# Gate and up products by Strassen's seven quarter products, with the activations kept in DRAM, in a two-layer diffusion block

## The chip, the cores and the metric

The kernel runs on one core of a Trainium2 chip. The core has a matrix engine (TensorE, PE in the views; its weight loads are PEld), a vector engine (DVE), a scalar engine (ACT), a third elementwise engine (GpSimd, POOL), a queue engine that issues transfers (SyncE, SP), a bank memory for matrix results (PSUM) and a scratch memory (SBUF). The metric is the device time of one launch in microseconds (us); lower is better.

## The reference, cut to what matters

Two layers on 512 latent tokens and 256 context tokens, D_MODEL 1024, D_FF 2816, all in float32. The change concerns the feed-forward part and what lies right before and behind it:

```python
for l in range(DEPTH):                       # 2 layers
    mod = silu_c @ w_ada[l] + b_ada[l]       # shift, scale, gate (twice each)
    ...                                      # norm, projections, two attentions, merge, output projection
    h2 = modulate(rms_norm(x, norm2_g[l]), sh2, sc2)
    x = x + gt2 * swiglu(h2, w_ffn_gate[l], w_ffn_up[l], w_ffn_down[l])
    if not last:
        ...                                  # the same for the context tokens, with the same weights
return rms_norm(x, final_norm_g)

def swiglu(h, w_gate, w_up, w_down):
    return (jax.nn.silu(h @ w_gate) * (h @ w_up)) @ w_down
```

In the second layer only the 512 latent tokens pass the feed-forward part; in the first all 768 do.

## The kernel before, in words

Features lie across partitions and tokens along the free dimension, so an activation is a list of tiles of 128 features by 768 (layer 0) or 512 tokens (layer 1). Every matrix operand is split into a high and a low part, and `mm3` (L564) makes each product of a 128x128 weight block with a piece of tokens from three matmuls: high tokens with low weights (L569), low with high (L570), high with high (L571). In the page the token operand is `hh, hl` (normed input) or `ah, al` (activation), the weights are `wh, wl`, the result bank is `d`.

Instructions are issued in the order in which the program emits them. `defer` (L160) puts an emission off until the matrix engine has been handed a given amount of further work, counted by `pe` (L155).

Weights come through `Weights` (L41): tiles of 128 output features by 1024 (or 896) inputs are loaded over SP's queue into one of three buffers with the tag `wf` (L60), split on ACT (`wh`, L70) and DVE (`wl`, L71); each `get` splits two tiles ahead and loads a third.

The modulation columns are worked out in the background. `ada` (L446) loads a 512 KB tile of w_ada, named `wa`, **into the same three `wf` buffers**, and leaves one or two dot products on DVE (L455, L456: one for the latent condition, a second one where the context needs it too). `background` (L169) issues the dots of the tile loaded last and then the load of the next, `rate` times for each weight tile; called with a count it empties the list. In layer 0's feed-forward part the list has 56 tiles with 80 dots.

The feed-forward part is the second half of `rest` (L1055). The norm before it is made in two token halves: statistics (`st`, `rv`, `rr`, `rb`), then for each of eight feature tiles a product on DVE (`t`, L520), scale and shift on POOL (L531), the high part on ACT (L536) and the low part on DVE (L539). `norm` (L542) spreads these steps over matrix work. Then D_FF is walked in three groups of 7, 7 and 8 feature tiles (`GROUPS`): for every tile 8 input tiles by gate and by up (`ev_gate`: silu on ACT, L1126; `ev_up`: product on DVE, L1129, then split, L176 and L177), and behind a group its share of the down products, one weight tile for each of 8 output tiles, added to the residual stream `x` in SBUF by DVE (L1084). The last group runs in two token halves, so that the norm of the next layer can begin. Token pieces are 384 wide in layer 0; in layer 1 they are 512 wide but for the first three jobs of the feed-forward part and the last down group, which go by 256.

Of the kernel before, what the change touches and what calls it, by code (L numbers as in the profile page):

```python
# [32 lines left out]
ADA_RATE = 0.35  # L33
EPS = 1e-6
# [6 lines left out]
class Weights:  # L41
    """Streams weight tiles from DRAM in the order of use and splits each into two F32R parts."""
# [71 lines left out]
def drain(gen):  # L114
    for _ in gen:
        pass


class Kernel:
# [33 lines left out]
    # Instructions are issued in the order they are emitted: work that waits for another engine  # L153
    # is put off until the tensor engine has been given enough else to do.
# [25 lines left out]
    def weight_order(self, l):  # L180
# [11 lines left out]
        for _ in range(2):  # L192
            for m in range(8):
                W.add(a["w_out"][l, m])
        for g, (f0, fn) in enumerate(GROUPS):
            for f in range(2 * f0, 2 * (f0 + fn)):
                W.add(a["w_gu"][l, f])
# [4 lines left out]
    def run(self):  # L202
        nc, a = self.nc, self.a
        self.xg = self.tc.dram_tile([16, P, TOK], F32, name="gate_scratch")
        self.xs = self.tc.dram_tile([KD, P, SEQ], F32, name="x_scratch")
# [26 lines left out]
        self.cos = self.const("cos", [P, SEQ])  # L232
        self.sin = self.const("sin", [P, SEQ])
        self.mask = self.const("mask", [P, 5 * P])
# [14 lines left out]
    def first(self, tiles, fourth):  # L249
        """The first norm of layer 0, its shift and scale (on the tensor engine, in halves of four  # L250
        feature tiles) and three weight tiles with the contraction outermost."""
# [15 lines left out]
        def follow(i):  # L267
# [4 lines left out]
            if i == len(parts) - 1:  # L272
                for t, src in ((self.cos, "cos"), (self.sin, "sin"), (self.mask, "mask")):
                    nc.sync.dma_start(out=t, in_=self.a[src])
# [171 lines left out]
    def ada(self, l, f, both):  # L446
        """One tile of 128 modulation features; returns the arithmetic, to be issued once the tile is there."""
# [11 lines left out]
    def ada_scale(self, l, j, s):  # L459
        """norm gain * (1 + scale), in place of the scale columns."""  # L460
# [4 lines left out]
    def square(self, k, c0, c1, eng=None):  # L465
        """Adds up the squares of the feature tiles; the last one may be left for stats() to add."""
# [15 lines left out]
    def rstd_cols(self, ps, n, width, out):  # L482
        """1 / sqrt(ps / width + eps) of [P, n] sums."""
# [5 lines left out]
    def stats(self, c0, c1):  # L489
        """1 / rms of the tokens c0..c1, tokens across partitions."""  # L490
# [11 lines left out]
    def spread(self, r, c0, c1):  # L502
        """The same, along the free dimension of every partition."""
# [38 lines left out]
    def norm(self, l, j, c0, c1, pace):  # L542
        """The same, spread over the tensor engine's next work."""
# [55 lines left out]
    def dense_first(self, tiles):  # L599
        """Three weight tiles, the early chunks of all of them first: tiles of (chunks, evac)."""  # L600
# [21 lines left out]
    def head_stats(self, sq, n, r):  # L622
        """1 / rms of each of two heads' 64 rows, tokens across partitions: r [P, tiles * 2]."""
# [643 lines left out]
```

## Time and profile before

| what | us |
|---|---|
| median of 3 runs (1930.03 to 1935.9) | 1931.82 |
| span of the profiled execution | 1932.0 |
| busy in it: PE / DVE / ACT / POOL | 1880.6 / 1169.8 / 847.7 / 523.7 |
| layer 0, feed-forward stretch looked at (600 to 1155): PE busy | 555.00 |
| layer 1, the same (1582 to 1904): PE busy | 322.00 |

The profiled execution lies 0.2 us from the median, so its times can be set against the runs as they are. A stretch in which PE is busy for its full length has no gap between matmuls; DVE, ACT and POOL then work beside it.

### The profile page before, as it was taken

How to read it: one execution, taken by the hardware profiler on the slowest of the kernel's cores; microseconds unless marked ns; L12 is line 12 of the kernel's file. 1: busy time of each engine (PE TensorE's matmuls, PEld its weight loads, DVE VectorE, ACT ScalarE, POOL GpSimd, SP SyncE). 2: the span in 40 equal slices, each digit the busy share in tenths (PEclk: the TensorE clock that was granted, in tenths of full speed). 3: DMA queues.
4: the chain of work that ended last, by engine and by line, in shares of the span. 5: the costliest groups of instructions: out<-in, count | busy, mean ns of one | idle time of the engine just before them, and what ended most of it. 6: DMA issues, size and time to landing. Idle time of an engine off the chain costs nothing.

```text
span 1932.0 us, 29203 instructions
## 1 busy us (share of the span) xinstructions
PE 1880.6 (97%) x11248; PEld 1758.6 (91%) x11248; DVE 1169.8 (61%) x2095; ACT 847.7 (44%) x1607; POOL 523.7 (27%) x568
## 2 busy tenths in 40 slices
PE   7999999999999999999999999999999999999998
PEld 3889899988999999999999998888889998888887
DVE  7668868996556567545444457676886653333344
ACT  5458745776334221221122334774885442222233
POOL 3436636562234000000000144654651320000003
PEclk8999999999999999999999999999999999999999
DMA  8232332224442434443433451212116533333334
GB/s 289 90 96 80 93 104 86 80 71 170 139 145 87 120 118 137 129 130 124 149 121 123 130 164 57 75 50 75 62 34 202 181 110 92 105 94 103 93 109 137
DMA packets 67739, 219.89 MB, mean 114 GB/s; under 512 B 7649, under 2 KB 9729, under 8 KB 67473
## 3 DMA queue, kind: packets, MB, share of 16 engines
q1 hardware_dynamic: 60416, 204.30, 34.1%
q10 hardware_dynamic: 6992, 13.64, 1.9%
q8 instruction: 89, 1.46, 0.3%
q0 software_dynamic: 192, 0.08, 0.1%
q14 instruction: 50, 0.40, 0.1%
HBM read 203.32 MB, written 14.68 MB: 113 GB/s over the span
## 4 chain that ended last, share of the span: by engine, by line
PE 73%; POOL 1%; DVE 1%; ACT 1%; issue 1%; POOLq 0%; ACTq 0%; DVEq 0%
PE d L570 20%; PE d L571 20%; PE d L569 20%; PE av L834 2%; PE pr L571 2%; PE pr L569 2%; PE pr L570 2%; PE pt L823 2%; PE S L759 1%; PE S L760 1%; POOL t L531 0%; PE st L497 0%; PE S L762 0%; PE S L763 0%; DVE wl L71 0%
## 5 line engine op out<-in xcount | busy, mean ns | idle before, releaser
L569 PE MATMUL d<-hh,wl 128*128 128x384 f32 (+2 forms) x1728 | 614.2, 355 | 0.6 <-DVE q L845 0.4
L570 PE MATMUL d<-hl,wh 128*128 128x384 f32 (+2 forms) x1728 | 603.1, 349 | 1.5 <-DVE hl L539 1.3
L571 PE MATMUL d<-hh,wh 128*128 128x384 f32 (+2 forms) x1728 | 602.6, 349 | 0.0
L71 DVE TENSOR_TENSOR wl<-wf,wh 128x1024 fp32r<-128x1024 f32 (+1 forms) x221 | 272.5, 1234 | 274.6 <-ACT wh L70 273.8
L70 ACT ACTIVATE wh<-wf 128x1024 fp32r<-128x1024 f32 (+1 forms) x255 | 265.6, 1042 | 283.2 <-PE d L571 176.3
L570 PEld LDWEIGHTS d<-hl,wh 128*128 128x128 f32 x1728 | 326.7, 189 | 19.2 <-DVE hl L539 3.2
L571 PEld LDWEIGHTS d<-hh,wh 128*128 128x128 f32 x1728 | 325.7, 188 | 19.9
L569 PEld LDWEIGHTS d<-hh,wl 128*128 128x128 f32 x1728 | 326.4, 189 | 17.8 <-issue 0.9
L480 POOL TENSOR_TENSOR ssq<-ssq,sq 128x384 f32<-128x384 f32 (+1 forms) x48 | 68.5, 1428 | 879.7 <-ACT sq L476 865.3
L569 PE MATMUL d<-ah,wl 128*128 128x384 f32 (+2 forms) x592 | 197.7, 334 | 0.0
L571 PE MATMUL d<-ah,wh 128*128 128x384 f32 (+2 forms) x592 | 197.4, 333 | 0.0
L570 PE MATMUL d<-al,wh 128*128 128x384 f32 (+2 forms) x592 | 197.4, 333 | 0.0
L455 DVE SCALAR_TENSOR_TENSOR junk<-wa,crow 128x1024 bf16<-128x1024 f32 x128 | 159.2, 1244 | 0.0
L808 POOL TENSOR_SCALAR p<-p,rec 128x768 f32<-128x768 f32 (+3 forms) x160 | 131.4, 834 | 94.7 <-DVE rec L805 65.8
L1084 DVE SCALAR_TENSOR_TENSOR x<-d,mod,x 128x384 f32<-128x384 f32 (+3 forms) x144 | 70.8, 510 | 135.3 <-PE d L571 135.3
L176 ACT ACTIVATE ah<-s 128x384 fp32r<-128x384 f32 (+2 forms) x68 | 37.4, 551 | 248.2 <-DVE s L1129 248.2
L864 DVE TENSOR_TENSOR pt<-pt,pt 128x512 fp32r<-128x512 f32 (+1 forms) x192 | 123.9, 661 | 25.3 <-ACT pt L860 23.9
L860 ACT ACTIVATE pt<-pt 128x512 fp32r<-128x512 f32 (+1 forms) x192 | 107.3, 577 | 32.2 <-PE pt L823 28.0
L823 PE MATMUL pt<-ident,p 128*128 128x128 f32 x736 | 110.7, 275 | 6.0 <-POOL p L808 3.2
L570 PEld LDWEIGHTS d<-al,wh 128*128 128x128 f32 x592 | 111.7, 189 | 4.4
L569 PEld LDWEIGHTS d<-ah,wl 128*128 128x128 f32 x592 | 111.7, 189 | 4.4
L1126 ACT ACTIVATE s<-d 128x384 f32<-128x384 f32 (+2 forms) x68 | 35.1, 517 | 183.5 <-PE d L571 183.4
(172 smaller groups left out, 3168.8 us busy)
## 6 DMA issues: line engine op xcount, KB each, us to landing
wa<-w_ada SPq DMA_DIRECT2D x96, 512.0 KB, 3.6
wf<-w_gu SPq DMA_DIRECT2D x88, 512.0 KB, 3.6
wf<-w_in SPq DMA_DIRECT2D x52, 512.0 KB, 3.6
wf<-w_out SPq DMA_DIRECT2D x32, 512.0 KB, 3.6
wf<-w_dn SPq DMA_DIRECT2D x32, 512.0 KB, 3.6
wf<-w_dn SPq DMA_DIRECT2D x32, 448.0 KB, 3.4
wf<-w_proj SPq DMA_DIRECT2D x16, 512.0 KB, 3.8
x<-x SPq DMA_DIRECT2D x16, 384.0 KB, 5.1
```

The lines of the kernel that those rows point to most:

```text
L70: high = lambda: self.nc.scalar.activation(hi[:, :n], t[:, :n], AF.Copy)
L71: low = lambda: (engine or (self.nc.vector if self.aux is None else self.nc.gpsimd)).tensor_tensor(lo[:, :n], t[:, :n], hi[:, :n], ALU.sub ...
L455: nc.vector.scalar_tensor_tensor(junk, t, 1.0, self.crow[:, s, :], ALU.mult, ALU.mult, accum_out=acc)
L480: (eng or nc.gpsimd).tensor_tensor(self.ssq[:, c0:c1], self.ssq[:, c0:c1], t[:, c0:c1], ALU.add)
L569: nc.tensor.matmul(ps, wl[:, ks], xh[:, c0:c1], start=first, stop=False)
L570: nc.tensor.matmul(ps, wh[:, ks], xl[:, c0:c1], start=False, stop=False)
L571: nc.tensor.matmul(ps, wh[:, ks], xh[:, c0:c1], start=False, stop=last)
L808: nc.gpsimd.tensor_scalar(pt, pt, rec[:, i:i + 1], 1.0, ALU.mult, ALU.mult)
L823: nc.tensor.transpose(ps[:, o:o + P], u["p", i][:, (j0 + j) * P:(j0 + j + 1) * P], self.ident)
L860: nc.scalar.activation(r[1][0], r[0], AF.Copy)
L864: nc.vector.tensor_tensor(r[1][1], r[0], r[1][0], ALU.subtract)
L1084: nc.vector.scalar_tensor_tensor(x[:, b0:b1], ps[:, b0 - c0:b1 - c0], self.mod[l][s][:, gate:gate + 1], x[:, b0:b1], ALU.mult, ALU.add)
```

## The change

For both layers (`FAST`), the gate and up products of one feature tile f are taken together as a 2x2 block product: rows gate and up, inner halves of 512 inputs, columns the two token halves. Strassen's scheme (in Winograd's form) needs seven quarter products in place of eight, and sums on both sides. The token side (T1 to T4) is made once in `norm_fast`, at the end of the norm's second half; the weight side (S1 to S4, named `S`, `wh/wl`, `sh/sl`, `zh/zl`) for every f on DVE, POOL and ACT; the results are combined from the banks on DVE and ACT. The matrix work of f is `q6, r7, q5, p1, p2, p3, r4`; for the first four f (`EARLY`) the two plain gate products come first, by `Weights`, the other five later. A quarter product is 4 inner blocks by 3 matmuls, 384 wide in layer 0 and 256 wide in layer 1.

The activation of each f is stored to DRAM (`act_scratch`), and so is `x` (`x_scratch`); all 22 f run before any down product. Then `down` loads `x` and the activations again, splits them, and runs the three down groups. `project` leaves `rate` at 0 and `gate_up` does not raise it; `down` sets it to 2 in layer 0. The emptying call ahead of the last group stays.

```diff
+FAST = (True, True)
+EARLY = 4
...
+        if FAST[l]:
+            for f in range(EARLY):
+                W.add(a["w_gu"][l, 2 * f])
...
+    def norm_fast(self, l, n, half, c0, c1):
...
+            t0 = self.t0
+            for i in (0, 4, 1, 5, 2, 6, 3, 7):
+                times(i, rb)
+                affine(i)
+            J = range(4)
+            for j in J:
+                nc.vector.tensor_tensor(t[j], t[j], t[j + 4], ALU.subtract)
+                nc.vector.tensor_tensor(t0[j], t[j], t0[j], ALU.subtract)
+                high("T2", j, t0[j])
+            for j in J:
+                low("T2", j, t0[j])
+                high("T3", j, t[j])
...
+            for j in J:
+                low("T4", j, t0[j + 4])
...
+    def gate_up(self, l, last, n, tq):
...
+        def prep_s(f):
+            if f < NF:
+                s = S[f]["S"] = self.xa.tile([P, 1024], F32, name=self.nm("S"), tag="S", bufs=1)
+                G, U = S[f]["G"], S[f]["U"]
+                nc.vector.tensor_tensor(s[:, :512], U[:, :512], U[:, 512:], ALU.add)
+                nc.vector.tensor_tensor(s[:, 512:], G[:, :512], U[:, :512], ALU.add)
+
+        def prep_s2(f):
+            if f < NF:
+                G, s = S[f]["G"], S[f]["S"]
+                nc.gpsimd.tensor_tensor(G[:, :512], G[:, :512], s[:, :512], ALU.add)
+                nc.gpsimd.tensor_tensor(G[:, 512:], G[:, 512:], G[:, :512], ALU.add)
...
+        first(0, 0)
+        for f in range(EARLY):
+            if f + 1 < EARLY:
+                first(f + 1, 0)
+            first(f, 1)
+        self.flush()
...
+            prep_s(0)
+            prep_s2(0)
+            prep_24(0)
+            load(2)
+            prep_13(0)
+            prep_s(1)
+            prep_s2(1)
+            prep_24(1)
+            q6(0)
+            r7(0)
+            ev_sum(0, "u")
...
+    def down(self, l, last, n, chunks, halves, streams):
+        nc = self.nc
+        self.xt = []
+        for m in range(8):
+            x = self.unit("x")
+            nc.sync.dma_start(out=x[:, :n], in_=self.xs[m][:, :n])
+            self.xt.append(x)
...
+        acts = []
+        for f in range(2):
+            load(f)
+        for f in range(GROUPS[0][1]):
+            load(f + 2)
+            ready(f)
+        self.rate = 0 if last else 2
+        for g, (f0, fn) in enumerate(GROUPS):
+            act, acts = acts[:fn], []
...
+            def step(m):
+                f = f0 + fn + m
+                if g + 1 < len(GROUPS) and m < GROUPS[g + 1][1]:
+                    load(f + 2)
+                    ready(f)
+            self.down_group(l, last, chunks, halves, streams, g == len(GROUPS) - 1, act, step)
```

Three places in the order of instructions, all in layer 0. First DVE at the end of the norm ahead of the feed-forward part. `t` is the scaled input tile, `hl` its low part, `wl55` the low part of the second weight tile behind that norm. Before:

```order
L520 TENSOR_TENSOR t_1361_6891<-x_1247_6217,rb_1346_6851 128x384
L539 TENSOR_TENSOR hl_1301_6575<-t_1359_6873,hh_1300_6574 128x384
L520 TENSOR_TENSOR t_1362_6900<-x_1251_6254,rb_1346_6851 128x384
L539 TENSOR_TENSOR hl_1307_6606<-t_1360_6882,hh_1306_6605 128x384
L1129 TENSOR_TENSOR s_1333_6793<-s_1333_6793,d_1345_6844 128x384
L177 TENSOR_TENSOR al_1335_6795<-s_1333_6793,ah_1334_6794 128x384
```

After (`H` is a part of a token-side sum; here the last four of 20 low parts; `wl55` now belongs to the fourth of the four early tiles, `S` is the weight-side sum of f = 0 and then f = 1):

```order
L1258 TENSOR_TENSOR H_1366_6962<-t_1305_6607,H_1366_6962 128x384
L1258 TENSOR_TENSOR H_1367_6966<-t_1307_6625,H_1367_6966 128x384
L1258 TENSOR_TENSOR H_1368_6970<-t_1312_6655,H_1368_6970 128x384
L1258 TENSOR_TENSOR H_1369_6974<-t_1314_6673,H_1369_6974 128x384
L73 TENSOR_TENSOR wl55_6988<-wf55_6826,wh55_6987 128x1024
L1351 TENSOR_TENSOR S_1374_7066<-rawU_1329_6799 128x512
L1352 TENSOR_TENSOR S_1374_7066<-rawG_1328_6797,rawU_1329_6799 128x512
L1337 TENSOR_TENSOR wl_1376_7072<-rawG_1328_6797,wh_1375_7071 128x1024
L1337 TENSOR_TENSOR sl_1380_7080<-S_1374_7066,sh_1379_7079 128x1024
L1351 TENSOR_TENSOR S_1381_7083<-rawU_1331_6803 128x512
```

Where norm steps and feed-forward steps alternated, all 44 DVE instructions of the norm's second half now stand in one piece ahead of `wl55` and of the first weight-side sum; ACT has its 20 high parts in one piece too, ahead of the silu of the first early tile and of `wh55`.

Second, SP where the down products begin. Before, the loads of down weights simply follow those of gate and up weights, each with one `wa` behind it:

```order
L60 DMA wf64_7467<-w_gu 128x1024
L450 DMA wa_1420_7477<-w_ada 128x1024
L60 DMA wf65_7542<-w_gu 128x1024
L450 DMA wa_1430_7552<-w_ada 128x1024
L60 DMA wf66_7610<-w_dn0 128x896
L450 DMA wa_1437_7620<-w_ada 128x1024
```

After, the last two stores of activations and the first loads of `x` (the loads of five further tiles follow):

```order
L1442 DMA act_scratch_79<-s_1744_9516 128x768
L1442 DMA act_scratch_79<-s_1761_9639 128x768
L1544 DMA x_1768_9725<-x_scratch_78 128x768
L1544 DMA x_1769_9727<-x_scratch_78 128x768
L1544 DMA x_1770_9729<-x_scratch_78 128x768
```

and behind the eight of `x` ten loads of activations (`ar`), here the last three of them, and then the next weights:

```order
L1551 DMA ar_1793_9775<-act_scratch_79 128x768
L1551 DMA ar_1796_9781<-act_scratch_79 128x768
L1551 DMA ar_1799_9787<-act_scratch_79 128x768
L62 DMA wf57_9797<-w_dn0 128x896
L62 DMA wf58_9803<-w_dn0 128x896
L62 DMA wf59_9809<-w_dn0 128x896
L453 DMA wa_1802_9811<-w_ada 128x1024
```

So 18 loads of 384 KB now stand between the last store and the next weight load.

Third, SP ahead of the last down group. Before:

```order
L60 DMA wf112_10647<-w_dn2 128x1024
L450 DMA wa_1744_10653<-w_ada 128x1024
L60 DMA wf113_10718<-w_dn2 128x1024
L450 DMA wa_1752_10724<-w_ada 128x1024
L60 DMA wf114_10782<-w_dn2 128x1024
L60 DMA wf115_10850<-w_dn2 128x1024
```

After, to the first rows of a row of loads that goes on:

```order
L62 DMA wf73_10887<-w_dn2 128x1024
L453 DMA wa_2000_10893<-w_ada 128x1024
L453 DMA wa_2003_10899<-w_ada 128x1024
L62 DMA wf74_10956<-w_dn2 128x1024
L453 DMA wa_2010_10962<-w_ada 128x1024
L453 DMA wa_2013_10968<-w_ada 128x1024
L453 DMA wa_2018_11021<-w_ada 128x1024
L453 DMA wa_2021_11027<-w_ada 128x1024
L453 DMA wa_2024_11033<-w_ada 128x1024
```

Two `wa` stand behind each down weight, none stands in `gate_up` any more, and the emptying call has 24 loads of `wa` left to issue (from `wa_2018` on) between `wf74` and `wf75`. They go to two buffers in turn, since `wf74` keeps the third until it is split.

## Rows read from the trace of the kernel before

**Rows 1.** The page: span, and PE's busy time, share and instructions.
```profile
span 1932.0 us, 29203 instructions
...
PE 1880.6 (97%) x11248; PEld 1758.6 (91%) x11248; DVE 1169.8 (61%) x2095; ACT 847.7 (44%) x1607; POOL 523.7 (27%) x568
```

**Rows 2.** Windows of both feed-forward stretches: length, busy time by engine, clock, DMA.
```profile
600.00:1155.00 555.00, 555.00 (x3218) 555.00 (x3217) 293.66 (x511) 135.22 (x201) 36.96 (x38) 1.00 0.41 127
...
1582.00:1904.00 322.00, 322.00 (x1545) 271.95 (x1544) 122.38 (x132) 91.66 (x117) 9.21 (x7) 1.00 0.35 104
```

**Rows 3.** Windows, L569 alone (a third of all matmuls there): length, its count.
```profile
605.90:717.10 111.20, 71.55 (x214) 40.15 (x214) 1.00 0.36 107
950.30:1083.20 132.90, 85.47 (x256) 47.86 (x255) 1.00 0.40 127
1460.16:1506.11 45.95, 36.17 (x128) 24.38 (x127) 1.00 0.65 212
...
1671.71:1747.64 75.93, 43.57 (x112) 20.83 (x111) 1.00 0.31 96
```

**Rows 4.** DVE's instruction groups, 600 to 1155: busy us, mean ns | idle before.
```profile
L455 DVE SCALAR_TENSOR_TENSOR junk<-wa,crow 128x1024 bf16<-128x1024 f32 x80 | 97.5, 1218 | 0.0
L71 DVE TENSOR_TENSOR wl<-wf,wh 128x1024 fp32r<-128x1024 f32 x61 | 74.7, 1225 | 105.2 <-ACT wh L70 105.1
L177 DVE TENSOR_TENSOR al<-s,ah 128x384 fp32r<-128x384 f32 x44 | 24.5, 558 | 26.1 <-ACT ah L176 26.1
...
L71 DVE TENSOR_TENSOR wl<-wf,wh 128x896 fp32r<-128x896 f32 x16 | 17.5, 1092 | 13.0 <-ACT wh L70 13.0
L1084 DVE SCALAR_TENSOR_TENSOR x<-d,mod,x 128x384 f32<-128x384 f32 x24 | 14.7, 615 | 14.4 <-PE d L571 14.4
```

**Rows 5.** ACT's instruction groups, same stretch.
```profile
L70 ACT ACTIVATE wh<-wf 128x1024 fp32r<-128x1024 f32 x61 | 64.3, 1053 | 70.7 <-PE d L571 49.8 <-issue 21.0
...
L536 ACT ACTIVATE hh<-t 128x384 fp32r<-128x384 f32 x16 | 8.3, 520 | 17.5 <-POOL t L531 17.5
...
L1126 ACT ACT_TABLE_LOAD x1 | 1.3, 1283 | 0.0
```

**Rows 6.** POOL's instruction groups, whole span.
```profile
L531 POOL TENSOR_SCALAR t<-t,mod 128x256 f32<-128x256 f32 x39 | 28.2, 725 | 6.9 <-DVE t L520 6.6
L617 POOL TENSOR_TENSOR rt<-q,cos 128x512 f32<-128x512 f32 x16 | 23.1, 1449 | 36.6 <-ACT q L641 18.1 <-ACT q L639 16.9 <-issue 1.6
...
L531 POOL TENSOR_SCALAR t<-t,mod 128x128 f32<-128x128 f32 x16 | 9.4, 589 | 6.7 <-DVE t L520 6.7
```

**Rows 7.** DVE's timeline at the norm ahead of layer 0's feed-forward part: start, us.
```profile
606.19 1.48 DVE L520 TENSOR_TENSOR t<-x,rb 128x384 f32<-128x384 f32 x3 [4.89 <-PE rb L506]
```

**Rows 8.** DVE's timeline at the same norm in layer 1.
```profile
1560.93 0.42 DVE L520 TENSOR_TENSOR t<-x,rb 128x256 f32<-128x256 f32 x1 [4.11 <-PE rb L506]
```

**Rows 9.** The page's DMA issues: count, KB each, median us from issue to landing.
```profile
wa<-w_ada SPq DMA_DIRECT2D x96, 512.0 KB, 3.6
...
x<-x SPq DMA_DIRECT2D x16, 384.0 KB, 5.1
```

**Rows 10.** A window in which transfers run at their densest: last columns DMA share, GB/s.
```profile
10.00:20.00 10.00, 7.18 (x12) 0.74 (x10) 6.84 (x7) 6.57 (x8) 0.00 (x0) 0.83 1.03 411
```

**Rows 11.** DVE's timeline in a down group, one weight tile with its dots.
```profile
725.82 1.09 DVE L71 TENSOR_TENSOR wl<-wf,wh 128x896 fp32r<-128x896 f32 x1 [0.29 <-ACT wh L70]
726.83 1.22 DVE L455 SCALAR_TENSOR_TENSOR junk<-wa,crow 128x1024 bf16<-128x1024 f32 x1
...
728.16 1.22 DVE L455 SCALAR_TENSOR_TENSOR junk<-wa,crow 128x1024 bf16<-128x1024 f32 x1
```

**Rows 12.** SP's waits, 600 to 1155: total us, times, longest.
```profile
SPq L450 <- DVE wl L71: 326.6, 56, 8.9
```

**Rows 13.** Windows round a gap of PE at 98 us: PE busy, ..., PEclk.
```profile
98.20:101.70 3.50, 1.52 (x10) 1.45 (x10) 2.92 (x10) 0.38 (x1) 0.00 (x0) 0.90 0.78 208
101.70:105.10 3.40, 3.40 (x21) 3.40 (x20) 0.00 (x0) 0.16 (x1) 0.00 (x0) 0.60 0.23 92
```

More of the change, by code (lines that the diff above doesn't have):

```diff
@@ L272, in follow @@
             if i == len(parts) - 1:
-                for t, src in ((self.cos, "cos"), (self.sin, "sin"), (self.mask, "mask")):
-                    nc.sync.dma_start(out=t, in_=self.a[src])
+                self.load_tables()
         def prep_tiles():
@@ L1050, in layer, with rest, merge @@
             self.hh = self.hl = self.Q = self.V = None
-        with tc.tile_pool(name="xp", bufs=8) as self.xp:
-            self.rest(l, last, n, chunks, halves, streams, Y)
-    def rest(self, l, last, n, chunks, halves, streams, Y):
+        return Y
+    def rest(self, l, Y):
+        nc, tc = self.nc, self.tc
+        last = l == DEPTH - 1
+        fast = FAST[l]
+        n = SEQ if last else TOK
+        chunks = [(0, 512)] if last else [(0, 384), (384, 768)]
+        halves = [(0, 256), (256, 512)] if last else chunks
+        streams = ((0, 0, SEQ), (1, SEQ, n))
+        with ExitStack() as es:
+            self.xp = es.enter_context(tc.tile_pool(name="xp", bufs=1, reuse_waits="tile"))
+            tq = ExitStack()
+            if fast:
+                self.tq = tq.enter_context(tc.tile_pool(name="tq", bufs=1, side="right", reuse_waits="tile"))
+            mt = self.merge(n, halves, Y)
+            self.project(l, last, n, halves, streams, mt)
+            mt = None
+            if not fast:
+                self.feed(l, last, n, chunks, halves, streams)
+        if fast:
+            with tc.tile_pool(name="xa", bufs=1, reuse_waits="tile") as self.xa:
+                self.gate_up(l, last, n, tq)
+            with tc.tile_pool(name="xp", bufs=1, reuse_waits="tile") as self.xp:
+                self.down(l, last, n, chunks, halves, streams)
+    def merge(self, n, halves, Y):
         nc = self.nc
@@ L1092, in load_x @@
                 x = self.unit("x")
-                src = self.a["x"][m] if l == 0 else self.xs[m]
+                src = self.a["x"][m] if l == 0 else self.xs[m][:, :n]
                 nc.sync.dma_start(out=x[:, :n], in_=src)
@@ L1140, in rest @@
                 act.append((hi, lo))
[L1141 to L1161 removed]
+            self.down_group(l, last, chunks, halves, streams, g == len(GROUPS) - 1, act)
@@ new lines, in feed, with down_group, evac @@
+        if last:
+            self.flush()
+    def down_group(self, l, last, chunks, halves, streams, end, act, step=lambda m: None):
+        nc = self.nc
+        if end and not last:
+            self.background(len(self.bg) + 1)
+            self.rate = 0
+            for s in range(2):
+                self.ada_scale(l + 1, 0, s)
+        for i, c in enumerate(halves if end else [chunks]):
+            for m in range(8):
+                def evac(ps, c0, c1, m=m):
+                    self.residual(l, streams, ps, self.xt[m], c0, c1, 40 + m)
+                    if end:
+                        self.defer(0.2, lambda: self.square(m, c0, c1))
+                        if i and not last:
+                            x = self.xt[m]
+                            self.defer(3.0, lambda: nc.scalar.dma_start(out=self.xs[m][:, :SEQ], in_=x[:, :SEQ]))
+                step(m)
+                drain(self.dense([c] if end else c, evac, act))
+            if end:
+                if last:
+                    self.final(*c, i == 1)
+                else:
+                    self.norm(l + 1, 0, *c, 0.5 if i else 2.0)
```

319 lines of the change are left out of this document (279 added, 40 removed).

## The prediction

> **What bounds the kernel now.** I read the page first: PE is busy for 97% of the span [rows 1], so either the amount of matrix work or a new gap in it moves the time. The windows of the two feed-forward stretches sharpen this: PE works through all of 555 us and all of 322 us, while DVE is busy for 53% and 38%, ACT and POOL for less [rows 2]. So fewer matmuls are worth their full time there, and every microsecond in which PE must wait for DVE, ACT, POOL or SP is paid in full. The windows of one matmul line give the pace. Each counts a third of the matmuls, so at width 384 one takes 111.20/(3x214) = 0.1732 and 132.90/(3x256) = 0.1730 us, at 256 45.95/384 = 0.1197, at 512 75.93/336 = 0.226 [rows 3].
>
> **What it removes.** Before, one f takes 2 x 8 inner blocks x 3 matmuls x 2 pieces = 96 matmuls, after it 7 x 4 x 3 = 84. Layer 0: 22 x 12 = 264 fewer at 0.1732, **-45.7 us**. Layer 1 trades widths: before, 192 of 256 columns (four half-width pieces of the first two f) and 960 of 512, 23.0 + 217.0 = 240.0; after, 1848 of 256, 221.2; **-18.8 us**. Two matmuls of 256 cost 0.239 against 0.226 for one of 512, which eats a good part of that layer's eighth. Down products are as many as before. Gain in all **64.5 us**.
>
> The Trainium skill, "TensorE: Matmul & The Clock Gate", section "Back-to-back issue gap", gives columns/2.4 GHz + 2.5 ns, that is 162.5, 109.2 and 215.8 ns. The trace has each some 10 ns longer, and the gain by the page would be 42.9 + 26.3 = 69 us.
>
> **What it adds, stage by stage** (all positive terms are time in which PE waits).
>
> *Norm to gate and up, layer 0.* `t` can begin at 606.19 [rows 7], right behind `rb`. Three of the early quarter products (12 matmuls, 2.08 us each) are then left that need nothing new; two others ran beside the deferrals of 2.2 and 2.0 us. PE thus stops at about 605.3 + 6.2 = 611.5. The next early tile needs a bank that the silu of the first one frees, and that silu stands on ACT behind 20 high parts; it also needs `wl55`, on DVE behind the 44 norm instructions. POOL takes 0.589 + 0.725 = 1.31 us for each of eight tiles [rows 6], so to 617; the 28 DVE instructions behind the last POOL tile take about 0.5 each (three `t` in 1.48, [rows 7]; 0.56 for a subtraction, [rows 4]), so to 632; table load, silu and high part on ACT (1.28 + 0.5 + 1.05, [rows 5]) fit before that; `wl55` takes 1.23 [rows 4]. PE goes on at 634: 22.5 us. Then the weight sums of f = 0: two DVE additions 1.3, two POOL additions of 512 columns at about 1.45 [rows 6], high part 1.05, low part 1.23, together 6.5 us against 6.2 us of early products, 0.7 late with the hand-over; and the copy `u(0)` stands on DVE behind the low part of S24(1), which needs another POOL-ACT-DVE chain, 4.2 us after r7(0). Sum **+28**. Bounds: 17 if only DVE's own 45 x 0.5 counts (POOL hidden), 34 if the DVE instructions are slowed beside POOL by a third.
>
> *The same in layer 1.* `t` begins at 1560.93 [rows 8], the POOL tiles take 8 x 0.73 [rows 6], the 28 instructions of 256 columns 0.42 each [rows 8], `wl55` follows at about 1580; PE has three products of 1.44, to 1564.5, so 15.5 us. Weight-side work does not shrink with the tokens while its cover does: q6(0) waits 4.5, `u(0)` 5.5, and for the next three f five products of 1.44 = 7.2 us face a chain of about 8.8, another 6. **+31** (20 to 40).
>
> *Later f.* Layer 0: 84 x 0.1732 = 14.5 us of PE for one f against about 9.5 of DVE, 6.3 of ACT and 4 of POOL: hidden. Layer 1: 10.1 us against a chain of about 10: **+2** (0 to 10).
>
> *Start of `down`.* SP is one queue in order. The last activation store waits for the last product and three DVE steps (1.7 us); 8 loads of `x` and 7 of activations of 384 KB must land before the seventh activation is split, and `wl56` stands behind the low parts on DVE. At 411 GB/s [rows 10] one takes 0.957 us, 15 take 14.4; with about 4 us for the first landing (5.1 for such a load in company, [rows 9]), the two splits (0.85 + 0.96, scaled from 0.52 and 0.56 at half the width) and 1.09 for `wl56` [rows 4] that is **+23** (16 to 28). PE has nothing else: r4(21) is the last work before. Layer 1, 256 KB: 15 x 0.64 = 9.6 and the same tail, **+17** (11 to 21).
>
> *Background at rate 2.* Before, the dots lay beside gate and up too. Now the 56 tiles stand only in layer 0's `down`, two behind each weight tile. The first of the two is loaded in the same call that dots it: SP issues it behind the next weight load, which waits for that `wl`, as the 56 `wa` do now [rows 12]; it lands 3.6 us later [rows 9], and DVE, in order, stands at its dot. So one weight tile costs DVE 0.87 (split of an activation) + 1.01 (`wl`, issue to issue, [rows 11]) + 3.65 + two dots at 1.34 (728.16 - 726.83, [rows 11]) + 1.25 (two residual pieces, [rows 4]) = 9.45 us for the 12 tiles with two dots, about 8.15 behind them; PE needs 42 x 0.1732 = 7.28. Over the 16 tiles of groups 0 and 1 DVE falls **22 us** behind, with the cover used up. Bounds 0 (no landing waited for: DVE then needs 5.8) and 30.
>
> *Emptying call before the last group.* 24 loads and 25 dots stand on SP and DVE ahead of `wl74`. Two buffers alternate, so load k+1 waits for dot k-1: two tiles in 3.6 + 0.1 + 1.34 = 5.0 us, 2.5 each, 60 us; then `wl74`, 1.23. PE's cover (jobs 72 and 73, 8.3 us) is mostly spent while DVE arrives late: **+62** less that overlap already counted above. Bounds: 25 if the dots run back to back (25 x 1.34 - 8.3), 70.
>
> The Trainium skill, "SBUF — State Buffer", section "The DMA setup-cost knee", has 2 us + bytes/436 GB/s, 3.2 us for 512 KB, where the trace shows 3.6; by it the call would take 56 us and the sum be 4 lower.
>
> *Clock.* After a gap of PE at 98 us the next 3.4 us ran at a granted clock of 0.60, mostly the lower of its two levels (1.2 and 2.4 GHz) [rows 13]; 3.4 x 0.4 = 1.4 us of work lost. Some five long gaps: **+8** (0 to 20).
>
> **Sum.** -64.5 + 28 + 31 + 2 + 23 + 17 + 22 + 62 + 8 = **+128.5**, on 1932.0 for the profiled execution, which stands 0.2 us over the median shown: **2060 us**. The lower ends together give +24, the upper +170; they are independent, so the range is 2010 to 2105. A difference of 0.3%, 6 us, is about what a measurement of this kernel can tell from no change.
>
> **Rivals.**
> 1. *The emptying call runs at DVE's pace* (25 us), since loads overlap dots in three buffers or land sooner. For it: dots in a down group of before follow each other without a gap [rows 11]. Against: there one load has a whole weight's time, 7 us, to land. About **2023 us**.
> 2. *The norm and `down` hand-overs are smaller*, and rate 2 costs nothing: lower ends there, the emptying call as forecast, -64.5 + 17 + 20 + 16 + 11 + 62 = +61: **1993 us**.
> 3. *Faster: the waiting tiles find cover.* If the `wa` loads run ahead, so that the background and the emptying call cost at most 10 us together, and both norms hide as now [rows 2], only the `down` starts remain: -64.5 + 27 + 10, **about 1905 us**. It decides at 64.5 us of waits; the busy shares of DVE speak for it (it has room for all the work), the written order against it.
> 4. *More clock loss and slower elementwise work*: upper ends of both norms, of layer 1's later f and of the clock, +6 + 9 + 8 + 12: **about 2095 us**.
> 5. *The products are not fewer in time*, because PE is held by the weight chain in each of the 18 later f of layer 1 (a period of 12 instead of 10.1 us): +34, **also about 2095 us**.
>
> **How the numbers follow.** Forecast (2035 to 2085) 0.55; rival 1 (2005 to 2035) 0.13; rival 2 (1938 to 2005) 0.08; rivals 4 and 5 together (above 2085) 0.19; within 0.3% 0.02; rival 3 and whatever else is faster 0.03. 2010 to 2105 leaves out a little of each outer case, about 0.2. Faster 0.03, same 0.02, slower 0.95.
>
> **What would show it.** Of layer 0's gate and up stretch, PE's windows should show about 320 us of work and gaps of 22 us where ACT works through `H` parts, then periods of 14.5 us without a gap. In `down`, PE should stand for some 20 us while SP moves at about 400 GB/s, then lose about 2 us a weight tile to a DVE that waits for `wa`, and then stand for 50 to 60 us with loads of `wa` 2.5 us apart. Layer 1 should be about even: -19 in matrix work against +50 in waits. The prediction is wrong if the emptying call is short, or if the norm's instructions are not what PE waits for.

## The result

The changed kernel takes 2104.37 us (median of 4 runs, 2102.96 to 2105.29) against 1931.74 for the kernel before in the same runs: ratio 1.0891, 95% interval 1.0875 to 1.0906. It is slower, as forecast, and lies at the very end of the range given (2010 to 2105), 0.6 us inside it and 44 us above the number given.

The page of the changed kernel, the lines that answer to [rows 1], and the granted clock in 40 slices:

```profile
span 2103.2 us, 31053 instructions
...
PE 1846.1 (88%) x11680; PEld 1752.2 (83%) x11680; DVE 1380.7 (66%) x2427; ACT 970.5 (46%) x1831; POOL 653.6 (31%) x656
...
PEclk8999999999989999997997699999999979999899
```

PE is busy 34.5 us less, and idle 257.1 us where it was idle 51.4. The matrix work removed is worth 64.5 us at the pace of [rows 3], so the matmuls that are left took 30 us longer in all. What PE waited for, from the view of waits (engine, line, releaser: total us, times, longest):

```profile
PE d L572 <- DVE wl L73: 112.1, 3, 67.9
PE a L1319 <- DVE wl L1337: 27.6, 21, 2.8
PE e L1319 <- DVE wl L73: 27.1, 2, 22.7
PE d L572 <- DVE x L1123: 14.5, 10, 2.8
PE e L1319 <- ACT s L1457: 13.3, 1, 13.3
...
PE a L1319 <- DVE u L1414: 5.3, 2, 3.3
```

Three waits for a low part of a down weight make 112 us: two at the start of the down stage, one ahead of the last group. The windows by stage say where each lies. In layer 0: the hand-over from the norm, early f, later f, start of `down`, groups 0 and 1, the emptying call, the last group (length, busy PE, PEld, DVE, ACT, POOL, clock, DMA share, GB/s):

```profile
601.90:648.00 46.10, 20.59 (x93) 19.86 (x91) 28.13 (x51) 17.04 (x31) 14.82 (x20) 0.70 0.30 114
648.00:690.00 42.00, 38.58 (x219) 37.87 (x218) 28.50 (x40) 12.97 (x17) 7.74 (x6) 1.00 0.34 113
690.00:953.50 263.50, 262.92 (x1513) 262.32 (x1511) 140.20 (x176) 102.70 (x159) 43.94 (x34) 1.00 0.25 90
953.50:978.00 24.50, 0.05 (x1) 0.00 (x0) 10.18 (x11) 7.58 (x9) 0.00 (x0) 0.57 0.90 342
978.00:1125.20 147.20, 132.56 (x720) 128.73 (x720) 121.34 (x244) 27.79 (x32) 0.00 (x0) 0.97 0.61 198
1125.20:1193.10 67.90, 0.01 (x1) 0.00 (x0) 36.27 (x80) 0.02 (x1) 0.00 (x0) 0.52 0.61 194
1193.10:1255.00 61.90, 61.90 (x355) 61.90 (x356) 36.59 (x53) 25.88 (x39) 26.23 (x21) 0.98 0.50 161
```

In layer 1, the hand-over, early f, later f, start of `down`, down groups:

```profile
1664.00:1700.00 36.00, 14.76 (x81) 13.85 (x79) 22.18 (x51) 12.26 (x29) 10.69 (x12) 0.72 0.35 122
1700.00:1740.00 40.00, 30.97 (x212) 30.05 (x213) 25.32 (x40) 12.40 (x17) 7.76 (x6) 0.86 0.31 105
1740.00:1945.70 205.70, 186.36 (x1518) 182.56 (x1516) 125.35 (x176) 92.94 (x159) 58.76 (x34) 0.99 0.30 104
1945.70:1965.50 19.80, 0.05 (x1) 0.00 (x0) 7.44 (x11) 6.05 (x10) 0.00 (x0) 0.62 0.85 298
1965.50:2092.00 126.50, 126.44 (x734) 112.56 (x734) 65.36 (x85) 43.59 (x61) 15.70 (x13) 0.98 0.46 148
```

Matmuls run slower where PE comes out of a gap: in layer 0's hand-over 93 of them took 20.59 us at a mean granted clock of 0.70, 0.221 each against 0.173 at the upper level.

In layer 0 the later f run without a gap (262.92 of 263.50); in layer 1 every one of them has one, 19 us in 206. The emptying call holds PE for 67.90 us with DVE busy for 36 of them, the clock granted near its lower level. SP and DVE in that call (timeline: start, us; the first row is 25 loads), then its loads from issue to landing (median us, from the view of DMA for 1125 to 1190):

```profile
1120.37 65.83 SPq L453 DMA_DIRECT2D wa<-w_ada  x25
...
1149.35 1.23 DVE L458 SCALAR_TENSOR_TENSOR junk<-wa,crow 128x1024 bf16<-128x1024 f32 x1 [1.25 <-DMA wa<-w_ada]
...
1152.19 1.22 DVE L458 SCALAR_TENSOR_TENSOR junk<-wa,crow 128x1024 bf16<-128x1024 f32 x1 [1.41 <-DMA wa<-w_ada]
...
1154.65 1.22 DVE L458 SCALAR_TENSOR_TENSOR junk<-wa,crow 128x1024 bf16<-128x1024 f32 x1 [1.04 <-DMA wa<-w_ada]
...
wa<-w_ada SPq DMA_DIRECT2D x23, 512.0 KB, 4.2
```

Each dot waits over 1 us for its load, where dots stood back to back before [rows 11], and they begin some 2.7 us apart. A load takes 4.2 us to land here, 3.6 before [rows 9]. The same wait marks groups 0 and 1 (978 to 1125): DVE waited there 16 times, 22.7 us in all, for a load of `wa`.

### The profile page after: what moved, and what is told of

Same layout as the page of the kernel before. It is cut to its first block, busy times and chain, and to the rows that moved or that the text cites. A ratio compares the mean times of both kernels' runs of the same rounds, so it can differ in the third digit from the quotient of the medians.

```text
span 2103.2 us, 31053 instructions
## 1 busy us (share of the span) xinstructions
PE 1846.1 (88%) x11680; PEld 1752.2 (83%) x11680; DVE 1380.7 (66%) x2427; ACT 970.5 (46%) x1831; POOL 653.6 (31%) x656
## 5 line engine op out<-in xcount | busy, mean ns | idle before, releaser
L73 DVE TENSOR_TENSOR wl<-wf,wh 128x1024 fp32r<-128x1024 f32 (+1 forms) x141 | 173.9, 1235 | 96.5 <-ACT wh L72 95.6
L572 PE MATMUL d<-hh,wl 128*128 128x384 f32 (+2 forms) x640 | 236.3, 369 | 0.6 <-DVE q L848 0.4
L573 PE MATMUL d<-hl,wh 128*128 128x384 f32 (+2 forms) x640 | 224.8, 351 | 0.9 <-DVE hl L542 0.9
L574 PE MATMUL d<-hh,wh 128*128 128x384 f32 (+2 forms) x640 | 224.5, 351 | 0.0
L1319 PE MATMUL a<-H,wh 128*128 128x384 f32 (+1 forms) x992 | 222.5, 314 | 0.0
L1319 PE MATMUL a<-H,wl 128*128 128x384 f32 (+1 forms) x496 | 158.9, 320 | 33.4 <-DVE wl L1337 27.6
L1337 DVE TENSOR_TENSOR wl<-rawG,wh 128x1024 fp32r<-128x1024 f32 x80 | 97.8, 1223 | 114.0 <-ACT wh L1336 113.9
L1319 PEld LDWEIGHTS a<-H,wh 128*128 128x128 f32 x992 | 171.5, 195 | 0.0
L574 PEld LDWEIGHTS d<-hh,wh 128*128 128x128 f32 x640 | 121.1, 189 | 7.6
L573 PEld LDWEIGHTS d<-hl,wh 128*128 128x128 f32 x640 | 122.2, 191 | 5.4 <-DVE hl L542 2.2
```

The costliest lines, as they stand in the source:

```text
L73: low = lambda: (engine or (self.nc.vector if self.aux is None else self.nc.gpsimd)).tensor_tensor(lo[:, :n], t[:, :n], hi[:, :n], ALU.sub ...
L572: nc.tensor.matmul(ps, wl[:, ks], xh[:, c0:c1], start=first, stop=False)
L573: nc.tensor.matmul(ps, wh[:, ks], xl[:, c0:c1], start=False, stop=False)
L574: nc.tensor.matmul(ps, wh[:, ks], xh[:, c0:c1], start=False, stop=last)
L1319: nc.tensor.matmul(ps, a[:, ks], b, start=first and j == 0 and i == 0, stop=j == 3 and i == 2, skip_group_check=True)
L1337: nc.vector.tensor_tensor(dst[1], src, dst[0], ALU.subtract)
```

## The experiments

Each one edits the changed kernel, whose trace is the one above.

**Is it the background's place?** The modulation tiles go into gate and up:

```diff
+            self.rate = 0 if last else 1
             for f in range(NF):
...
+                if not mixed:
+                    self.background()
+                    if 17 <= f <= 20:
+                        self.background()
                 load(f + 3)
...
-        self.rate = 0 if last else 2
+        self.rate = 0 if last else 1
```

> Edit: in layer 0 the modulation tiles are spread over gate and up (rate 1, called twice in each later f, three times in f 17 to 20), and run at rate 1 in the down stage, so that the emptying call ahead of the last group has no load left. Theory (background tiles put in the way of down weights on DVE and SP): the 68 us stand before the last group and the 22 us lost in groups 0 and 1 both go, gate and up keep their period of 14.5 us since DVE has room there: 2104 - 90 = 2014 us, 2005 to 2025. Rival (groups 0 and 1 are held by the loads and splits of the activations themselves, or DVE has no room in gate and up): 20 us stay in groups 0 and 1 or come back in gate and up, 2035 us or more.

Measured: **2015.61 us**, ratio to the kernel before 1.0433 (1.0417 to 1.0449): 89 us less. Windows of the later f and of everything from the first down product to the middle of the last group:

```profile
690.00:953.50 263.50, 262.92 (x1511) 262.23 (x1511) 246.03 (x367) 103.17 (x158) 68.87 (x34) 1.00 0.50 172
980.30:1135.60 155.30, 155.30 (x881) 155.30 (x881) 88.42 (x149) 39.61 (x48) 9.54 (x6) 0.98 0.50 170
```

DVE does 106 us more in the later f (246 against 140) and PE's 262.92 does not move; the down groups have no gap left. So the background cost nothing where matrix work covers it, and 89 us where it stood.

**How much does one load in the call cost?** The opposite, 16 more loads in it:

```diff
         for g, (f0, fn) in enumerate(GROUPS):
             act, acts = acts[:fn], []
+            if g == 1:
+                self.rate = 0
```

> Edit: on the changed kernel, rate 0 in down group 1 of layer 0, so that 40 loads of modulation tiles in place of 24 stand in the emptying call ahead of the last group. Theory (two buffers in turn, a load waits for the dot before last: 68 us for 24 loads, 2.75 each): 16 more cost 44 us, group 1 gives back the 9 us that it loses beside the background, 2104 + 35 = 2139 us, 2130 to 2148. Rival (the call runs at DVE's pace of 1.34 us for a dot behind a fixed start): 16 more cost 21, 2116 us, 2108 to 2124.

Measured: **2133.03 us** (1.1045, 1.1029 to 1.1062), 29 more than the changed kernel, within the theory's range (2130 to 2148) and outside the rival's (2108 to 2124). PE's longest wait and SP in that call:

```profile
PE d L572 <- DVE wl L73: 150.9, 3, 108.5
...
1108.43 106.56 SPq L453 DMA_DIRECT2D wa<-w_ada  x39
```

The wait grew by 108.5 - 67.9 = 40.6 us for 16 loads. The time alone hardly decides, since the rival was priced too low: 8 of the 16 extra tiles carry two dots, so the call has 50 dots in place of 25, and 25 more at 1.34 us are 33.5 us, not 21; less the 9 us that group 1 was to give back that is about 2129 us. The rows of DVE decide: between 1132 and 1220 us 32 dots, one for each load, begin 2.78 us apart, and every one of them waits for its load (42.2 us in all). That is half of a landing of 4.2 us and a dot of 1.34, as two buffers in turn ask, not the 1.34 us of a dot.

**Do the layers add up?** Only `FAST` is changed.

```diff
-FAST = (True, True)
+FAST = (True, False)
```

> Edit: FAST = (True, False), the seven products in layer 0 alone. Theory (the loss is a sum of the stages' own waits): layer 1's feed-forward part goes back from 427.9 us in the changed kernel's trace to 359.9 in that of the kernel before, 68 less: 2036 us, 2025 to 2045. Rival (layers are coupled, so that a part of layer 0's cost shows only with both): off by more than 10 us from that.

Measured: **2037.65 us** (1.0543, 1.0523 to 1.0563). And the other way:

```diff
-FAST = (True, True)
+FAST = (False, True)
```

> Edit: FAST = (False, True), the seven products in layer 1 alone. Theory: layer 0 gives back its 104 us (653.1 us from the first early product to the last down product, against 546.2 from the first gate product before, which begins 4 us later): 2000 us, 1990 to 2010, still slower than before by the 68 us of layer 1. Rival: layer 1 breaks even or gains by itself (fewer matmuls, little background), 1935 us or less.

Measured: **1996.10 us** (1.0333, 1.0315 to 1.0351). Both came out as expected. Layer 0 costs 106 and layer 1 64 us over the kernel before, 170 together against 172.6 for both: the layers are as good as independent, and layer 1 loses without any background work.

**What sets the period of a later f in layer 1?** The additions for S2 and S4 move from POOL to DVE:

```diff
-                nc.gpsimd.tensor_tensor(G[:, :512], G[:, :512], s[:, :512], ALU.add)
-                nc.gpsimd.tensor_tensor(G[:, 512:], G[:, 512:], G[:, :512], ALU.add)
+                nc.vector.tensor_tensor(G[:, :512], G[:, :512], s[:, :512], ALU.add)
+                nc.vector.tensor_tensor(G[:, 512:], G[:, 512:], G[:, :512], ALU.add)
```

> Edit: the two additions that make S2 and S4 run on DVE in place of POOL. Theory (in layer 1 each f is one serial chain DVE, ACT, DVE, POOL, ACT, DVE of 11.4 us, in which the two POOL additions take 1.3 + 2.15): DVE does both in about 1.3, the chain falls below PE's 10.1, the period of 18 later f falls to 10.1 to 10.3, -20 us, and each hand-over to gate and up wins a few us: 2078 us, 2065 to 2085. Rival (DVE's load is what sets the period): 1.3 us more of it for each f makes layer 1 as slow or slower, 2100 us or more.

Measured: **2068.48 us** (1.0709, 1.0693 to 1.0725), 36 less, as the theory expected and against the rival. First the changed kernel, one period in layer 1 (timeline, DVE, then ACT, then POOL):

```profile
1799.36 1.23 DVE L1337 TENSOR_TENSOR wl<-rawG,wh 128x1024 fp32r<-128x1024 f32 x1 [2.28 <-ACT wh L1336]
1800.50 0.42 DVE L1409 TENSOR_TENSOR s<-b,s 128x256 f32<-128x256 f32 x1
...
1802.35 1.22 DVE L1337 TENSOR_TENSOR wl<-rawG,wh 128x1024 fp32r<-128x1024 f32 x1 [1.10 <-ACT wh L1336]
...
1805.30 0.69 DVE L1352 TENSOR_TENSOR S<-rawG,rawU 128x512 f32<-128x512 f32 x1
...
1807.17 1.32 DVE L1337 TENSOR_TENSOR sl<-S,sh 128x1024 fp32r<-128x1024 f32 x1 [0.85 <-ACT sh L1336]
1810.77 1.22 DVE L1337 TENSOR_TENSOR wl<-rawG,wh 128x1024 fp32r<-128x1024 f32 x1 [2.28 <-ACT wh L1336]
...
1800.95 0.42 ACT L1420 ACTIVATE s<-s 128x256 f32<-128x256 f32 x1 [1.36 <-DVE s L1409]
1801.27 1.04 ACT L1336 ACTIVATE wh<-rawG 128x1024 fp32r<-128x1024 f32 x1
...
1809.68 1.06 ACT L1336 ACTIVATE wh<-rawG 128x1024 fp32r<-128x1024 f32 x1 [2.27 <-POOL rawG L1358]
...
1806.12 1.29 POOL L1357 TENSOR_TENSOR rawG<-rawG,S 128x512 f32<-128x512 f32 x1 [7.89 <-ACT w L1416]
1807.49 2.16 POOL L1358 TENSOR_TENSOR rawG<-rawG 128x512 f32<-128x512 f32 x1
```

Read in order of time this is one chain, each link beginning within about 0.1 us of the one before it: `wl` of one weight sum (1799.36), a sum `s` on DVE behind it (1800.50), the activation of that `s` on ACT (1800.95), `wh` of the next gate weight, which stands behind it on ACT (1801.27), its `wl` (1802.35), three more steps that DVE has ahead of the sum `S` (to 1805.99), POOL's two additions (to 1809.65), `wh` on ACT, the next `wl` at 1810.77. It closes in 11.41 us, where PE has 84 x 0.1197 = 10.05 of work [rows 3]. And the second POOL addition takes 2.16 us beside DVE's `sl`; with DVE idle, in layer 0, it took 1.27:

```profile
632.74 1.27 POOL L1358 TENSOR_TENSOR rawG<-rawG 128x512 f32<-128x512 f32 x1
```

The later f with both additions on DVE (one window):

```profile
1735.00:1905.00 170.00, 170.00 (x1429) 170.00 (x1428) 144.10 (x203) 89.58 (x152) 0.00 (x0) 1.00 0.34 121
```

PE has no gap left, with DVE busier than before (85% against 61%). The order of dependent steps over three engines was the bound, not the load of any. Of the 36 us, PE's idle time gave 25 (257.1 to 231.9) and faster matmuls 11 (busy 1846.1 to 1834.8).

**The start of `down`.** Activations first, `x` as it is needed, the first down weight split ahead of the activations:

```diff
+        for f in range(GROUPS[0][1]):
+            load(f)
+        self.W.split(self.W.at)
+        for f in range(GROUPS[0][1]):
+            ready(f)
+        load_x(0)
+        load_x(1)
...
             def step(m):
+                if g == 0:
+                    load_x(m + 2)
```

> Edit: at the start of the down stage the seven activations of the first group are loaded first, the first down weight is split before them, and the tiles of x are loaded one job at a time as they are needed. Theory (PE waits 24.5 us and 19.8 us there for 15 transfers in a row on one queue and for a low part queued behind them): PE begins about 7 us after the last product, when the first activation has landed and is split, and waits some 4 us more for the second weight: 24.5 becomes 11, 19.8 becomes 9, 2104 - 24 = 2080 us, 2072 to 2090. Rival (the wait is the latency of store and load behind the last product, not the number of transfers): both waits stay above 18 us, 2098 us or more.

Measured: **2094.53 us** (1.0838, 1.0823 to 1.0853), 10 less; neither number (2072 to 2090, and 2098 or more). The gap in layer 0, the first job with the wait behind it, then the next (windows); then SP's first loads of activations:

```profile
958.70:965.10 6.40, 0.00 (x0) 0.00 (x0) 2.52 (x4) 0.84 (x1) 0.00 (x0) 0.79 0.60 203
965.10:982.00 16.90, 11.55 (x42) 9.02 (x42) 8.71 (x9) 7.79 (x10) 0.00 (x0) 0.70 0.86 332
982.00:1000.00 18.00, 17.96 (x92) 17.96 (x93) 14.60 (x29) 4.02 (x6) 0.00 (x0) 0.88 0.75 255
...
960.78 3.45 SPq L1553 DMA_DIRECT2D ar<-act_scratch  x7
```

PE begins after 6.4 us in place of 24.5, but the first job of 42 matmuls (7.3 us at the upper clock level) takes until 982.0 with the wait for its successor's weight: it is fed by one landing after another, at a granted clock of 0.70. Much of the wait went from in front of the job into it, and over the run nearly half of the gain was lost again: PE's idle time fell by 18 us (257.1 to 239.4), but its matmuls took 8 us longer (busy 1846.1 to 1853.9). The loads begin 2 us after PE has stopped at 958.7, since SP stood 10.9 us at the last store, waiting for the last activation.

**The norm.** Its sums are emitted in the order of use, between the early products (step 0 makes T2, step 1 its low parts and T3, step 2 the low parts of T3 and T1); S2 and S4 of the first two f are made on DVE too:

```diff
+        for f in range(EARLY):
+            if f + 1 < EARLY:
+                first(f + 1, 0)
+            if f == EARLY - 2:
+                prep_24(0)
+                self.steps[0]()
+            first(f, 1)
+            if f == EARLY - 2:
+                self.steps[1]()
+                load(2)
+                prep_13(0)
+        q6(0)
+        self.steps[2]()
+        r7(0)
...
```

> Edit: at the norm ahead of gate and up, the token-side sums are emitted in the order in which the products use them (T2, T3, T1, 22, T4) and in pieces between the early products, the weight-side sum of f = 0 ahead of them; S2 and S4 of the first two f are made on DVE. Nothing is left out. Theory (PE waits 29 and 30 us there because the silu, the next weight's low part and the first weight-side sum stand behind all 44 norm instructions on DVE and 20 on ACT): PE waits only for the group of sums that it uses next, 10 to 14 us in each layer: 2104 - 33 = 2071 us, 2062 to 2084. Rival (the amount of DVE work there, some 50 instructions, sets the end in whatever order): 8 us less at most, 2095 us or more.

Measured: **2086.50 us** (1.0799, 1.0784 to 1.0814), 18 less: half of what the theory had, and neither number (2062 to 2084, and 2095 or more). PE's waits of the two kinds that it was about:

```profile
PE a L1333 <- DVE wl L1351: 29.8, 21, 4.3
...
PE e L1333 <- DVE wl L73: 7.2, 2, 4.3
```

The waits in the early products shrank from 27.1 to 7.2 us and the 13.3 for the silu went. Of the waits for weight sums (27.6 before) 18.9 stand in the later f of layer 1, which this edit leaves alone; they say nothing on it. At the hand-overs others came in: for the token-side sums `H` themselves 2.8 us in layer 0 and 5.4 in layer 1, for combined results (`w`) 4.0 and 6.4. Here too part of the gain was lost again: PE's idle time fell by 25 us (257.1 to 231.9), its matmuls took 5 longer (busy 1851.5).

**All four together**, with S2 and S4 on DVE in layer 1 only and for the first two f of layer 0:

> Edit: the four edits together in both layers (background spread over gate and up; S2 and S4 on DVE in layer 1 and for the first two f of layer 0; the new start of down; the new order at the norm). Theory (the waits are separate and add up): 2104 - 88 - 28 - 24 - 33 = 1931 us, 1918 to 1942, even with the kernel before. Rival (the waits removed reappear at the next late engine, DVE above all): 1945 us or more.

Measured: **1960.50 us** (1.0140, 1.0124 to 1.0157), 144 less. The theory is missed by 29 us, and the time lies where the rival had it (1945 or more). Of the 173 us expected the single edits had given 89 + 36 + 10 + 18 = 153, and together they gave 9 less than that, in part because e_s2dve and e_seam both move the additions of the first two f. The same with layer 1 as before:

> Edit: as the four edits together, with the seven products in layer 0 alone. Theory: 2037.7 for layer 0 alone, less 88 for the background, 12 for the start of down, 15 for the norm: 1922 us, 1912 to 1930, faster than the kernel before, since in layer 0 a product of width 384 has the cover that one of 256 lacks. Rival: as above, 1935 us or more.

Measured: **1931.22 us**, ratio 0.9992 (0.9983 to 1.0000): no difference that can be told from none, 9 us above the theory and below the rival.

**A second step on the two short ones.** The last activation goes out over POOL's queue, so that SP is free; the next down weights are loaded among the activations; S of f = 0 stands behind the fourth early weight, that of f = 1 is made on POOL:

```diff
-                nc.sync.dma_start(out=self.acts[f][:, :n], in_=s)
+                (nc.gpsimd if f == NF - 1 else nc.sync).dma_start(out=self.acts[f][:, :n], in_=s)
...
+            load(f)
+            if f == 3:
+                self.W.load(at + 1)
+        self.W.load(at + 2)
...
+        prep_s(1, nc.gpsimd)
```

> Edit: e_all_l0 with a better start of down (the last activation is stored over POOL's queue, so that SP is free for the loads of activations and of the next two down weights while PE still works) and at the norm the weight-side sum of f = 0 behind the fourth early weight, that of f = 1 on POOL. Theory (what was left were the 10 us behind the last product, a first down job fed by landings, 2.9 us before the fourth early product and 4.4 us before q6(1)): 1931 - 18 = 1913 us, 1905 to 1921, faster than before. Rival (the loads cannot start earlier since their buffers come free only with the last product): 1924 us or more.

Measured: **1919.74 us**, ratio 0.9942 (0.9930 to 0.9955): 0.6% faster than the kernel before, 7 us short of the number expected and within its range. Windows of layer 0 (hand-over, the other f, start of `down`, down groups), then SP's first loads of activations:

```profile
603.00:650.00 47.00, 34.47 (x151) 30.55 (x150) 39.38 (x61) 19.41 (x34) 21.42 (x22) 0.78 0.40 138
650.00:940.00 290.00, 288.20 (x1653) 286.67 (x1651) 264.38 (x391) 113.27 (x171) 74.45 (x39) 1.00 0.50 165
940.00:960.00 20.00, 14.57 (x66) 12.77 (x66) 11.79 (x16) 9.31 (x13) 0.63 (x1) 0.91 0.94 345
960.00:1139.00 179.00, 178.07 (x1033) 178.07 (x1034) 110.24 (x186) 52.35 (x70) 26.47 (x21) 1.00 0.57 186
...
939.03 2.09 SPq L1581 DMA_DIRECT2D ar<-act_scratch  x4
```

The loads begin while PE still works, and the start of `down` now costs 5 us of idle time, where e_start left 12; the hand-over still costs 12 and runs at a clock of 0.78. How much each of the three changes gave was not tried by itself. Both layers so:

> Edit: the same in both layers. Theory: e_all less twice what the layer gains above, less 2 for the shorter tiles of layer 1: 1960.5 - 32 = 1928 us, 1918 to 1938; layer 1 still costs more than it saves, so that this stays above e_best_l0. Rival: layer 1 turns into a gain, below e_best_l0.

Measured: **1945.14 us**, 1.0070 (1.0056 to 1.0083), 17 us above the number expected and outside its range (1918 to 1938): the edits of this step gave layer 0 11 us and layer 1 only 4. Layer 1 still adds 25 us to e_best_l0, so the rival, a gain in layer 1, is refuted. Its hand-over and early f, then its later f:

```profile
1540.40:1620.00 79.60, 57.72 (x373) 54.21 (x372) 58.46 (x105) 30.72 (x56) 13.00 (x14) 0.81 0.41 142
1620.00:1797.50 177.50, 177.03 (x1484) 176.63 (x1482) 147.19 (x207) 92.23 (x158) 0.00 (x0) 1.00 0.35 122
```

The later f have no gap; 22 us of idle time and a mean clock of 0.81 stand in the first 80 us, more than the 18.8 us of work that the products save there.

**Where the time went in each run.** The span of the profiled execution against that of the kernel before (1932.0), split by the pages: matrix work removed at the pace of [rows 3]; time in which PE is idle beyond the 51.4 us of before; and what is left of PE's busy time, that is, matmuls that took longer than at that pace.

| run | work removed | more idle | slower matmuls | sum |
|---|---|---|---|---|
| changed kernel | -64.5 | +205.7 | +30.0 | +171.2 |
| e_bg | -64.5 | +120.1 | +26.0 | +81.6 |
| e_s2dve | -64.5 | +180.5 | +18.7 | +134.7 |
| e_start | -64.5 | +188.0 | +37.8 | +161.3 |
| e_seam | -64.5 | +180.5 | +35.4 | +151.4 |
| e_all | -64.5 | +55.4 | +35.6 | +26.5 |
| e_best | -64.5 | +48.6 | +26.9 | +11.0 |
| e_best_l0 | -45.7 | +20.6 | +11.1 | -14.0 |

In e_all the slower matmuls alone are more than the 26.5 us that it lies above the kernel before.

## Why the prediction was right, and where it was short

The direction, the places of the waits and the size of most of them were right. That the range held is partly luck: the time lies 0.6 us inside it, outside the band of the forecast itself (2035 to 2085, chance 0.55) and in that of rivals 4 and 5 (above 2085, 0.19). The upper ends of the terms add up to +188.5, not to the +170 written; the measured +171.2 would lie well inside the range that follows from that.

Term by term, the prediction's against the trace (gaps of PE summed in each place; the later f of layer 1 and groups 0 and 1 by their length):

| step | predicted | read |
|---|---|---|
| hand-over, layer 0 (gaps 22.7 + 2.8 + 2.0 + 1.4) | 28 | 28.9 |
| hand-over and early f, layer 1 (seven gaps of 1.1 to 13.3) | 31 | 30.0 |
| later f, layer 1: 18 x (11.41 - 10.05) | 2 | 24.5 |
| start of `down`, layers 0 and 1 | 23 + 17 | 24.5 + 19.8 |
| groups 0 and 1: 147.2 - 124.8 | 22 | 22.4 |
| emptying call | 62 | 67.9 |
| rest (clock) | 8 | 17.7 |

With the 64.5 us of saved work the rows above the last give 153.5, and the span grew by 171.2. The remainder of 17.7 us is no idle time: the idle parts of the rows (19.3 in the later f of layer 1, 14.6 in groups 0 and 1, and the other rows whole) make 205 of the 205.7 us by which idle time grew. It is slower matmuls, 30 us in all, of which 7.8 stand in groups 0 and 1 and 4.7 in the later f of layer 1, inside the rows above. Of the rest, 4.5 us stand in layer 0's hand-over (granted clock 0.70) and 10.7 in layer 1's hand-over and early f (0.72 and 0.86). In these three windows the clock was low; that it explains all of the 30 us was not shown.

*What bounds the kernel, and the gain.* PE was the bound, and later f without a gap ran at the pace foreseen in layer 0.

*The step that was short* is "Later f ... Layer 1: 10.1 us against a chain of about 10: **+2** (0 to 10)". The chain was seen, and mis-sized: 11.4 us, so that 18 f cost 24.5 us, half of the 44 that the forecast was short. The prediction does not list the links of its 10. The additions on POOL were put beside a multiplication of 1.45 us [rows 6], 2.9 for two; they took 1.29 and, beside a DVE subtraction of two SBUF tiles, 2.16. The other 0.9 us lie in links to which it gives no price, such as the one from a `wl` over an activation on ACT to the next gate weight. Rival 5 named this mechanism, at 12 us a period, but joined to a chance with rival 4; e_s2dve shows that it is the chain and not DVE's load.

The Trainium skill, "SBUF — State Buffer", section "SBUF: two separate sides", says that a DVE instruction with two SBUF inputs and a GpSimd instruction that reads SBUF exclude each other for a whole instruction. The trace agrees: POOL's addition, begun at 1807.49 while `sl` ran until 1808.49, took 0.87 us more than the one ahead of it.

*Two smaller steps.* The clock was put at 1.4 us for each of five long gaps, +8; the remainder is 17.7, and a single hand-over (layer 0) lost 4.5. The emptying call was put at 62 and took 67.9: its loads landed in 4.2 us, not in the 3.6 of [rows 9], and (4.2 + 0.1 + 1.34)/2 = 2.82 for 24 loads makes 67.7.

*Layer 1.* "About even", under what would show it, does not follow from the prediction's own sum, -19 + 50 = +31. Alone it cost 64 us (e_l1only), and its terms hold most of the shortfall.

*The page's pace.* The formula that the prediction takes from the Trainium skill, "TensorE: Matmul & The Clock Gate", section "Back-to-back issue gap", is given there for a single matmul by itself, not for a stream of weight loads and matmuls. So the 69 us are no forecast of that page; the sum does not use them.

*The background terms* were right in mechanism and nearly in size: e_bg takes both away (89 us for 22 + 68), and the rows of the call and of e_call40 show a dot every 2.7 to 2.8 us, each waiting for its load, not every 1.34. Rival 1 is refuted.

*The start of `down`* was right in size, but its picture (15 transfers in a row) was only half of it: e_start took the eight transfers of `x` out of the way, and of the 44 us of waits some 22 stayed, in part since SP issues no load before the store of the last activation, which waits for it. e_best_l0, which takes that store off SP and loads the next weights earlier, shortened the idle time in layer 0 to some 5 us.

*The norm* was right in size. In layer 0 the wait of 22.7 us was forecast as 22.5. Its last link was not DVE's, as the prediction had it, but ACT's:

```profile
628.82 1.23 DVE L73 TENSOR_TENSOR wl<-wf,wh 128x1024 fp32r<-128x1024 f32 x1 [1.46 <-ACT wh L72]
```

DVE was done with the norm's low parts 1.5 us before; the weight's high part stood on ACT behind 20 `H` parts, a table load and a silu. In layer 1 too the longest wait (13.3) is for the silu on ACT. Emitting both engines' steps in the order of use took 15 of the 29 us in layer 0 and 7 of 30 in layer 1; the two additions moved to DVE in the same edit have a part in it that was not tried by itself.

## What to carry to other kernels

A saving in matrix work is only the first term: ask for every piece of work that lay beside it where it goes when the stages are separated, and price it in the stage to which it moves. Work that was free in the background became 89 us of path when it moved to a stage with less cover and shared buffers. A gap in front of the matrix engine also cost more than its length here: the matmuls behind the gaps ran slower, 30 us in all in the changed kernel. And before halving the width of a product, check that the width-independent preparation of one step still fits under it: at 384 columns the scheme could be made to pay (0.6%), at 256 none of the versions tried did.

## What the runs showed of the hardware

The pace of [rows 3] holds in the changed kernel where PE has no gap: 1513 matmuls of 384 columns in 262.92 us (0.174 each), and in e_s2dve 1429 of 256 columns in 170.00 (0.119), so two halves cost more than the whole (0.226 for 512 [rows 3]). Behind a gap, at a mean granted clock of 0.70, a matmul of 384 columns took 0.221 us.

An addition of 512 columns on POOL took 1.27 us with DVE idle and 2.16 us beside a DVE subtraction of two SBUF tiles; on DVE an addition of that size took 0.69. A load of 512 KB landed in 4.2 us (median) in the emptying call and in 3.6 before, and with two buffers in turn and a dot of 1.34 us behind each load the loads went at 2.7 to 2.8 us each.
